# Moving the right-hand SBUF pools by 128 bytes and reordering the join between the two feed-forward products

## The chip, the cores and the metric

The kernel runs on one core of one Trainium2 chip. The metric is the device time of one execution, in microseconds. Three runs of the kernel before took 2131.59, 2133.08 and 2135.07 us; their median is 2133.08 us. The profiled execution was a run of its own: it took 2139.03 us, with a span of 2137.2 us from the first to the last instruction and a mean granted TensorE clock of 0.988.

## The reference

One layer of a decoder trunk over 512 positions and 2048 channels, all in float32: a conditioned RMSNorm, a mixer of three branches (causal pooling, forgetting attention with 8 heads, a gated linear recurrence), a residual; then a second conditioned RMSNorm, a gated feed-forward part with a causal convolution of width 3, a residual, and a last RMSNorm. Cut to what matters here:

```python
h = rmsnorm(x, g_ffn) * (1.0 + sc2) + sh2
g = causal_dwconv(h @ w_ffn_gate, ffn_conv_w, ffn_conv_b)   # 2048 -> 5632
a = silu(g) * (h @ w_ffn_up)                                # 2048 -> 5632
x = x + gt2 * (a @ w_ffn_down)                              # 5632 -> 2048
return rmsnorm(x, final_g)
```

## The kernel before

Channels lie on the 128 partitions, the 512 positions on the free axis. D is 16 tiles of 128 channels, the feed-forward width 44 tiles (NFF). Each float32 product is made of three matmuls of a rounded high part and a low part (mm3, lines 111 to 114): high weight by high data, high weight by low data, low weight by high data. So every weight tile that a DMA brings is split first: ScalarE (ACT) writes the high part, VectorE (DVE) the low one (split_w, lines 98 to 104).

**Stages.** (1) start(): the first norm while the conditioning weights stream in, and the first products, whose weight tiles raw_s hold several column groups side by side: columns from 0 for zs, the column group from SA = 416 (1664 bytes) for zb and zc, and for the later half of the channels a second part, split into a tile of its own, again for zc. (2) A list of slots run by drive() (line 247): each slot loads one weight tile two slots ahead, splits it one slot ahead and multiplies 16 channel tiles, 48 matmuls of 512 columns: queries and keys (z_q, z_k), values (zv, 256 columns), the output projection (z_o), and the first four gate and up tiles (z_b, z_g, z_u). (3) strassen(): feed-forward tiles 4 to 43, each as seven half-size products of 8 channel tiles with 256 columns (pair_steps, line 974), software-pipelined: the steps of tile p carry the end of tile o before it (results c21, c11, c12, then conv0, conv, silu, gated, store). Each gated tile is written to DRAM (a_d). (4) The second product down: four groups of 9, 13, 9 and 13 gated tiles (FFG), each group 16 slots. A slot multiplies its group's tiles (27 or 39 matmuls of 512 columns; in the last group twice 39 of 256) and adds the result to the residual x1 (down_done, line 1066). The gated tiles come back from DRAM (load_a into four ar buffers) and are split into the pool fa (split_a, line 1083). The first slot of the group has its weight split in one piece (FirstDown, tiles fd_raw, fd_h, fd_l).

**Memory.** Pools with side "right" are laid from the top of the partition downwards, the others from the bottom upwards. On the right lie, from the top: pad (32 bytes, which take 64), then in stages 1 and 2 xy and wp (raw weights and their halves wh, wl); in stage 3 in their place q, ring (the halves of the Strassen weights) and sm; in stage 4 fa (the halves of the gated tiles). On the left lie hp (the halves hh, hl of the normed data), the Strassen forms t3 and t42, mp (convolution results cv and gated tiles ac), and in stage 4 fd, wq (the weights of down and their halves), ar and xq (x1). By the addresses that the program gives them, all large left tiles start 64 bytes above a multiple of 256, all large right tiles 192 above one. A pool that takes the place of another is opened with reuse_waits="tile": a new tile waits for the last readers of the old tiles under it.

**What orders the work.** Each engine works through its own list in order. The lists come from a scheduler of the framework that simulates the program, so two instructions of one engine can change places against the text of the kernel where neither needs the other. All loads and stores are issued by one engine's queue (SyncE, SP), in order too: an issue that waits holds up those behind it.

**The join.** At the end of strassen() the chain of the last tile runs: c12 after the last product, conv0 (ACT), two conv steps (DVE), silu (ACT), gated (DVE), store (SP). Then the pools of stage 3 are closed, those of stage 4 opened, and the program reads:

```python
down[0].once("load")
raws = [load_a(i) for i in range(4)]
down[0].once("split0")
for i in range(FFG[0]):
    split_a(0, i, raws.pop(0))
    if i + 4 < FFG[0]:
        raws.append(load_a(i + 4))
for j in range(KC):
    x1[j] = xy.tile([P, S], F32, tag="xy", name=f"x1b_{j}")
    nc.sync.dma_start(x1[j], x1_d[j])
```

Of the kernel before, what the change touches and what calls it, by code (L numbers as in the profile page):

```python
# [10 lines left out]
F32 = mybir.dt.float32  # L11
# [5 lines left out]
P = 128  # L17
D = 2048
S = 512
KC = D // P  # L20
DFF = 5632
NFF = DFF // P
# [27 lines left out]
def trunk(ctx: ExitStack, tc: tile.TileContext, xT, c_d, pack_d, small_w, w_ada, w_s0, w_s1, w_b, w_z, w_v, w_o, w_gu, w_dn, out):  # L50
    nc = tc.nc
# [5 lines left out]
    def pool(stack, name, bufs, side="left"):  # L57
        return stack.enter_context(tc.tile_pool(name=name, bufs=bufs, side=side, reuse_waits="tile"))

    hp = pool(hps, "hp", 16)  # L60

    pool(ctx, "pad", 1, "right").tile([P, 8], F32, name="pad")
    xy = pool(rps, "xy", 16, "right")
    wp = pool(rps, "wp", 3, "right")
    dr = ctx.enter_context(tc.tile_pool(name="dr", bufs=1, space=bass.MemoryType.DRAM))
# [8 lines left out]
    def par(name, i=0, n=1):  # L74
        a = PACK[name][0] + i
        return pk[:, a:a + n]
# [12 lines left out]
    x1_d = [dr.tile([P, S], F32, name=f"x1_d{j}") for j in range(KC)]  # L89
# [81 lines left out]
    class Norm:  # L171
# [21 lines left out]
        def sum(self):  # L193
            nb = self.n // P
            s2 = bank(f"s2_{self.name}")

            for n, t in enumerate((self.acc, self.sq)):
                for b in range(nb):
                    T.matmul(s2[:, b:b + 1], t[:, b * P:(b + 1) * P], ones[:, 0:1], start=n + b == 0, stop=n == 1 and b == nb - 1)
            v, q, r = (self.tp.tile([P, 4], F32, tag=f"n{n}", name=f"{n}_{self.name}")[:, 0:nb] for n in "vqr")  # L200
            A.activation(q, s2[:, 0:nb], AF.Sqrt, bias=epsc, scale=1.0 / D)
            V.tensor_scalar(v, s2[:, 0:nb], 1.0 / D, EPS, op0=ALU.mult, op1=ALU.add)
            V.reciprocal(r, q)

            V.tensor_tensor(q, r, r, ALU.mult)
            V.tensor_tensor(q, q, v, ALU.mult)
            V.tensor_scalar(q, q, -0.5, 1.5, op0=ALU.mult, op1=ALU.add)
            V.tensor_tensor(r, r, q, ALU.mult)
            self.d = self.tp.tile([P, 4, P], F32, tag="d", name=f"d_{self.name}", bufs=1)[:, 0:nb]
            V.tensor_tensor(self.d, ident.unsqueeze(1).broadcast_to([P, nb, P]), r.unsqueeze(2).broadcast_to([P, nb, P]), ALU.mult)  # L210
# [36 lines left out]
    def drive(slots):  # L247
        def ahead(i, what):
            if i < len(slots):
                slots[i].once(what)  # L250

        ahead(0, "load")
        ahead(1, "load")
        ahead(0, "split0")
        ahead(0, "split1")
        yield
        for i, s in enumerate(slots):
            ahead(i + 2, "load")
            ahead(i + 1, "split0")
            if sum(x.n <= 1024 for x in slots[i:i + 3]) == 3:  # L260
                ahead(i + 3, "load")
                ahead(i + 2, "split0")
            for n in range(max(s.ada, 1)):
                if n < s.ada:
                    next(bg, None)
                ahead(i + 1, "split1")
            s.mm(s)
            for f in s.pe:
                f()
            for f in s.post:  # L270
                f()
# [382 lines left out]
    def later(f, *a):  # L654
        return lambda: f(*a)
# [60 lines left out]
    x1 = [None] * KC  # L716
    tm = Branches()
# [52 lines left out]
    def store_a(i, a):  # L770
        nc.sync.dma_start(a_d[i], a)
# [65 lines left out]
    def form1(c):  # L837

        v, h, l = x1[c][:, LO], g_h[c][:, HI], g_l[c][:, HI]
        A.copy(h, v)  # L840
        V.tensor_tensor(l, v, h.bitcast(F32), ALU.subtract)
# [11 lines left out]
    slots[-2].pe += [later(forms, c) for c in todo]  # L853


    sps = ExitStack()
    st = Branches()

    def strassen_start():

        rps.close()
        st.q = pool(sps, "q", 1, "right")
        st.r = pool(sps, "ring", 4, "right")
        st.m = pool(sps, "sm", 2, "right")
        f = st.first = Pair(PLAIN)
        f.load_a()
        f.load_b()
        f.sum1()
        f.high("a11")
        f.sum2()  # L870
        f.low("a11")
        f.high("s2")
        f.sum3()
        for c in range(HC):
            form1(c)

    class Pair:
# [10 lines left out]
        def load_a(self):  # L888
            self.load_part("a11", 0, 0, 1)
            self.load_part("a21", 1, 0, 2)  # L890
            self.load_part("a22", 1, 1, 2)
# [52 lines left out]


        def conv0(self):
            self.t = tm.m.tile([P, S], F32, tag="t", name=f"cv{self.i}")
            A.activation(self.t, self.g, AF.Identity, bias=par("fcb", self.i), scale=par("fcw", 3 * self.i + 2))

        def conv(self, s):  # L950
# [4 lines left out]
            A.activation(self.t, self.t, AF.Silu)  # L955

        def gated(self):
            self.a = tm.m.tile([P, S], F32, tag="a", name=f"ac{self.i}")
            V.tensor_tensor(self.a, self.u, self.t, ALU.mult)

    def b_of(j0, c):
# [12 lines left out]
    def pair_steps(p, q, o):  # L974

        A_, B_, C_, D_ = None, None, None, None
        q.load_a()
        A_ = p.half("A")
        p.product(A_, "a11", b11, True)
        p.high("s1")  # L980
        p.low("s2")
        o.c21()
        o.c11()

        o.last()
        m1 = p.kept("m1", A_)
        p.high("s3")
        p.low("s1")
        o.gated2()

        p.product(A_, "s2", T2, False)
        p.high("a12")
        o.c12()
        p.low("s3")
        o.conv0()
        o.conv(1)
        o.store2()

        C_ = p.half("C")
        p.product(C_, "s1", t1, True)  # L1000
        u2 = p.kept("u2", A_)
        p.high("a22")
        o.conv(2)
        o.silu()
        p.low("a12")
        p.sum4()

        p.product(A_, "s3", T3, False)
        q.load_b()
        q.high_a11()  # L1010
        p.low("a22")
        q.sum1()
        o.gated()

        B_ = p.half("B")
        p.product(B_, "a12", b21, True)
        u3 = p.kept("u3", A_)
        p.high("s4")
        q.sum2()
        q.low_a11()  # L1020
        o.store()

        D_ = p.half("D")
        p.product(D_, "a22", T4, True)
        q.high_s2()
        p.result("u", HI, u3, C_)
        p.low("s4")
        q.sum3()

        def last():  # L1030
            p.product(C_, "s4", b22, False)
        p.last = last
        p.c21 = lambda: p.result("u", LO, u3, D_)
        p.c11 = lambda: p.result("g", LO, m1, B_)
        p.c12 = lambda: p.result("g", HI, u2, C_)
        p.gated2 = p.store2 = lambda: None
        p.store = lambda: store_a(p.i, p.a)

    ABSENT = Absent()
# [2 lines left out]
    Pair.high_s2 = lambda self: self.high("s2")  # L1042

    def strassen():
        o, p = ABSENT, st.first
        for i in range(PLAIN, NFF):
            q = Pair(i + 1) if i + 1 < NFF else ABSENT
            pair_steps(p, q, o)
            o, p = p, q
        o.c21()  # L1050
        o.c11()
        o.last()
        o.c12()
        o.conv0()
        o.conv(1)
        o.conv(2)
        o.silu()
        o.gated()
        o.store()


    a_h, a_l = {}, {}
    down = []
# [19 lines left out]
    def split_a(g, i, a):  # L1083
        t = tm.fa.tile([P, 2, S], F32R, tag=f"a{g % 2}", name=f"a{i}", bufs=FFG[g])
        A.copy(t[:, 0], a)
        V.tensor_tensor(t[:, 1], a, t[:, 0].bitcast(F32), ALU.subtract)
        a_h[i], a_l[i] = t[:, 0], t[:, 1]
# [57 lines left out]
    for _ in stream:  # L1145
        pass
    strassen_start()
    strassen()

    sps.close()  # L1150
    fps.close()
    hps.close()
    ops = ExitStack()
    tm.fd = pool(ops, "fd", 1)
    wp = pool(ops, "wq", 3)
    tp = pool(ops, "tq", 2)
# [1 line left out]
    xy = pool(ops, "xq", 16)  # L1158
# [3 lines left out]
        norms[3, i] = Norm(tp, HALVES[i], f"n3{i}")  # L1162
    down_slots()
    stream = drive(down)
    down[0].once("load")
    raws = [load_a(i) for i in range(4)]
    down[0].once("split0")
    for i in range(FFG[0]):
        split_a(0, i, raws.pop(0))
        if i + 4 < FFG[0]:  # L1170
            raws.append(load_a(i + 4))
    for j in range(KC):
        x1[j] = xy.tile([P, S], F32, tag="xy", name=f"x1b_{j}")
        nc.sync.dma_start(x1[j], x1_d[j])
    for _ in stream:
        pass
    fas.close()
    n = norms[3, 1]
    n.sum()
    n.spread()  # L1180
    with tc.tile_pool(name="op", bufs=1, side="right", reuse_waits="tile") as op:
        o = op.tile([P, KC, S // 2], F32, name="o")
        for j in range(KC):
            V.scalar_tensor_tensor(o[:, j], x1[j][:, n.c], par("final_g", j), n.r, op0=ALU.mult, op1=ALU.mult)
            if j + 1 in OUT_CUTS:
                a = OUT_CUTS[OUT_CUTS.index(j + 1) - 1]
# [66 lines left out]
```

## Time and profile before

| | |
|---|---|
| median of three runs | 2133.08 us |
| profiled execution | 2139.03 us, span 2137.2 us |
| TensorE (PE) busy | 2064.7 us, 97% of the span |
| weight loads of PE (PEld) busy | 1858.5 us, 87% |
| VectorE (DVE) busy | 1503.1 us, 70% |
| ScalarE (ACT) busy | 862.3 us, 40% |
| DMA | 354.59 MB, mean 166 GB/s |
| Strassen stage | about 801 to 1604 us |
| second product | about 1614 to 2121 us |

Matmuls are pipelined, so the duration of one in the profile is longer than the distance from its start to the next one's start; the pace is the distance between starts. Times in the views are microseconds from the span's start. In a timeline the bracket behind an instruction tells how long its engine sat idle before it, and what released it.

### The profile page before, as it was taken

The page shows a single profiled execution, that of the slowest core. Times are in us where ns is not written, and L with a number is a line of the kernel's source. Part 1 is how long each engine was busy: PE and PEld are TensorE (multiplying, and loading weights), DVE is VectorE, ACT ScalarE, POOL GpSimd, SP SyncE. Part 2 cuts the span into 40 slices and gives each one's busy share as a digit, 9 for nine tenths or more (in the row PEclk, how much of TensorE's full clock was granted, in tenths as well). Part 3 has the DMA queues.
Part 4 walks back from the last instruction along what each step waited for, and adds up shares of the span by engine and source line. Part 5 has one row for each costly group of instructions (what it writes and reads, how often), then busy time and mean ns, then how long its engine had stood idle before and what let it go on. Part 6 is the DMA issues. An engine that isn't in the chain of part 4 may idle for free.

```text
span 2137.2 us, 31894 instructions
## 1 busy us (share of the span) xinstructions
PE 2064.7 (97%) x13172; PEld 1858.5 (87%) x13172; DVE 1503.1 (70%) x1901; ACT 862.3 (40%) x1196; POOL 29.5 (1%) x51
## 2 busy tenths in 40 slices
PE   5899999999999899999999999999997999999997
PEld 3678888988888689999999999999995888888997
DVE  7987876676677848888888888888865342343675
ACT  4247433235222634444444444444444231222442
POOL 0001100002000000000000000000000000000000
PEclk9999999999999899999999999999998999999998
DMA  9962465556888314443443443343328342333563
GB/s 360 363 232 90 177 225 210 217 217 220 287 308 304 107 55 143 124 126 108 124 130 106 121 133 107 120 131 109 123 65 293 103 157 89 94 123 109 189 210 129
DMA packets 86212, 354.59 MB, mean 166 GB/s; under 512 B 9393, under 2 KB 13617, under 8 KB 68529
## 3 DMA queue, kind: packets, MB, share of 16 engines
q1 hardware_dynamic: 86066, 352.55, 49.1%
q8 instruction: 103, 1.69, 0.3%
q14 instruction: 43, 0.35, 0.1%
HBM read 332.59 MB, written 19.92 MB: 165 GB/s over the span
## 4 chain that ended last, share of the span: by engine, by line
PE 86%; DVE 5%; DMA 5%; issue 2%; ACT 2%; SPq 0%; POOL 0%; DVEq 0%; ACTq 0%; POOLq 0%
PE z_d L112 8%; PE z_d L114 8%; PE z_d L113 8%; PE A L929 5%; PE A L928 5%; PE A L930 5%; PE C L928 4%; PE C L929 4%; PE C L930 4%; DMA raw_ada<-in_w_ada 3%; PE D L929 2%; PE B L929 2%; PE D L928 2%; PE B L928 2%; PE B L930 2%
## 5 line engine op out<-in xcount | busy, mean ns | idle before, releaser
L112 PE MATMUL z_d<-a,wh_d 128*128 128x512 f32 (+1 forms) x903 | 310.8, 344 | 4.1 <-ACT wh_d L102 4.1
L113 PE MATMUL z_d<-a,wh_d 128*128 128x512 f32 (+1 forms) x903 | 310.1, 343 | 0.0
L114 PE MATMUL z_d<-a,wl_d 128*128 128x512 f32 (+1 forms) x903 | 310.1, 343 | 0.0
L103 DVE TENSOR_TENSOR wl_d<-raw_d,wh_d 128x896 fp32r<-128x896 f32 (+3 forms) x158 | 145.1, 919 | 159.5 <-ACT wh_d L102 158.9
L102 ACT CAST wh_d<-raw_d 128x896 fp32r<-128x896 f32 (+3 forms) x158 | 127.0, 804 | 319.5 <-PE z_d L113 312.9
L112 PEld LDWEIGHTS z_d<-a,wh_d 128*128 128x128 f32 x903 | 170.2, 189 | 26.9 <-ACT wh_d L102 4.6
L114 PEld LDWEIGHTS z_d<-a,wl_d 128*128 128x128 f32 x903 | 170.1, 188 | 22.7 <-DVE wl_d L103 0.4
L113 PEld LDWEIGHTS z_d<-a,wh_d 128*128 128x128 f32 x903 | 170.3, 189 | 22.3
L125 DVE SCALAR_TENSOR_TENSOR raw_ada<-raw_ada,crep 128x2048 f32<-128x2048 f32 x64 | 146.4, 2288 | 60.5 <-DMA raw_ada<-in_w_ada 60.3
L1066 DVE SCALAR_TENSOR_TENSOR x1b<-z_d,mod,x1b 128x512 f32<-128x512 f32 (+1 forms) x80 | 51.5, 644 | 96.0 <-PE z_d L114 95.9
L928 PE MATMUL C<-hh_b,s1h 128*128 128x256 f32 x320 | 90.2, 282 | 2.9 <-ACT s1h L914 2.9
L930 PE MATMUL A<-hh_b,a11l 128*128 128x256 f32 x320 | 90.2, 282 | 1.7 <-DVE a11l L919 1.7
L928 PE MATMUL A<-t42h,s2h 128*128 128x256 f32 x320 | 90.1, 282 | 0.0
L929 PE MATMUL A<-t42l,s2h 128*128 128x256 f32 x320 | 90.1, 281 | 0.0
L928 PE MATMUL C<-hh_b,s4h 128*128 128x256 f32 x320 | 90.1, 281 | 0.0
L930 PE MATMUL C<-hh_b,s1l 128*128 128x256 f32 x320 | 90.0, 281 | 0.0
L928 PE MATMUL A<-t3h,s3h 128*128 128x256 f32 x320 | 90.0, 281 | 0.0
L929 PE MATMUL A<-t3l,s3h 128*128 128x256 f32 x320 | 90.0, 281 | 0.0
L930 PE MATMUL A<-t3h,s3l 128*128 128x256 f32 x320 | 90.0, 281 | 0.0
L928 PE MATMUL B<-hh_b,a12h 128*128 128x256 f32 x320 | 90.0, 281 | 0.0
L929 PE MATMUL B<-hl_b,a12h 128*128 128x256 f32 x320 | 90.0, 281 | 0.0
L930 PE MATMUL B<-hh_b,a12l 128*128 128x256 f32 x320 | 90.0, 281 | 0.0
(637 smaller groups left out, 6172.5 us busy)
## 6 DMA issues: line engine op xcount, KB each, us to landing
a<-in_w_gu SPq DMA_DIRECT2D x160, 512.0 KB, 3.9
raw_ada<-in_w_ada SPq DMA_DIRECT2D x64, 1024.0 KB, 5.2
raw_d<-in_w_dn SPq DMA_DIRECT2D x48, 832.0 KB, 4.4
ada<-in_w_ada SPq DMA_DIRECT2D x32, 1024.0 KB, 7.2
raw_d<-in_w_dn SPq DMA_DIRECT2D x31, 576.0 KB, 3.8
raw_o<-in_w_o SPq DMA_DIRECT2D x16, 1024.0 KB, 5.0
a_d<-ac SPq DMA_DIRECT2D x44, 256.0 KB, 3.8
ar<-a_d SPq DMA_DIRECT2D x44, 256.0 KB, 3.9
```

The lines of the kernel that those rows point to most:

```text
L102: A.copy(h, raw[:, a:b])
L103: V.tensor_tensor(l, raw[:, a:b], h.bitcast(F32), ALU.subtract)
L112: T.matmul(acc, wh, xh, start=start, stop=False)
L113: T.matmul(acc, wh, xl, start=False, stop=False)
L114: T.matmul(acc, wl, xh, start=False, stop=stop)
L125: V.scalar_tensor_tensor(raw, raw, 1.0, crep, op0=ALU.mult, op1=ALU.mult, accum_out=modr[:, n:n + 1])
L928: T.matmul(o, wh[:, w], xh, start=first, stop=False, skip_group_check=True)
L929: T.matmul(o, wh[:, w], xl, start=False, stop=False, skip_group_check=True)
L930: T.matmul(o, wl[:, w], xh, start=False, stop=last, skip_group_check=True)
L1066: V.scalar_tensor_tensor(x1[j][:, c], acc[:, c], mod[:, 80 + j:81 + j], x1[j][:, c], op0=ALU.mult, op1=ALU.add)
```

## The change

The padding tile at the top of the right side grows from 32 to 160 bytes (64 to 192 as laid out), which puts xy, wp and fa 128 bytes lower against a multiple of 256. A pool end (three tiles of 2048 bytes: g, u and t of the last feed-forward tile) is opened on the right ahead of the Strassen pools and stays open to the end of stage 4, and a second pad of 128 bytes lies below it during stage 3, so that q, ring and sm are 6400 bytes lower than before, 25 times 256. The last tile's gated result is written over its convolution tile t. strassen() ends with the last product and its results; the rest of the last chain (conv0 to store) is called after the loads and splits of the second product's first slots. The second slot's load and splits, and the third slot's load, are called among the splits of the first nine gated tiles. Four of the 16 residual tiles are loaded ahead of the last chain, and each of the other twelve at the end of a slot, three slots ahead of its use.

```diff
-    pool(ctx, "pad", 1, "right").tile([P, 8], F32, name="pad")
+    pool(ctx, "pad", 1, "right").tile([P, 40], F32, name="pad")
...
-    sps = ExitStack()
+    sps, ops = ExitStack(), ExitStack()
...
         rps.close()
+        st.end = pool(ops, "end", 1, "right")
+
+        pool(sps, "pad2", 1, "right").tile([P, 32], F32, name="pad2")
         st.q = pool(sps, "q", 1, "right")
...
         def conv0(self):
-            self.t = tm.m.tile([P, S], F32, tag="t", name=f"cv{self.i}")
+            if not hasattr(self, "t"):
+                self.t = tm.m.tile([P, S], F32, tag="t", name=f"cv{self.i}")
...
         def gated(self):
-            self.a = tm.m.tile([P, S], F32, tag="a", name=f"ac{self.i}")
+            self.a = tm.m.tile([P, S], F32, tag="a", name=f"ac{self.i}") if self.i + 1 < NFF else self.t
...
             q = Pair(i + 1) if i + 1 < NFF else ABSENT
+            if q is ABSENT:
+                for n in "gut":
+                    setattr(p, n, st.end.tile([P, S], F32, name=f"last_{n}"))
             pair_steps(p, q, o)
             o, p = p, q
+        o.last()
+        o.c11()
         o.c21()
-        o.c11()
-        o.last()
         o.c12()
-        o.conv0()
-        o.conv(1)
-        o.conv(2)
-        o.silu()
-        o.gated()
-        o.store()
+        return o
...
+    def load_x1(j):
+        x1[j] = xy.tile([P, S], F32, tag="xy", name=f"x1b_{j}")
+        nc.sync.dma_start(x1[j], x1_d[j])
+
     down[0].once("load")
     raws = [load_a(i) for i in range(4)]
     down[0].once("split0")
+    down[1].once("load")
     for i in range(FFG[0]):
         split_a(0, i, raws.pop(0))
         if i + 4 < FFG[0]:
             raws.append(load_a(i + 4))
-    for j in range(KC):
-        x1[j] = xy.tile([P, S], F32, tag="xy", name=f"x1b_{j}")
-        nc.sync.dma_start(x1[j], x1_d[j])
+        if i == 2:
+            down[2].once("load")
+        if i == 4:
+            down[1].once("split0")
+            down[1].once("split1")
+    for j in range(4):
+        load_x1(j)
+    for f in (last_pair.conv0, later(last_pair.conv, 1), later(last_pair.conv, 2), last_pair.silu, last_pair.gated, last_pair.store):
+        f()
+    for j in range(4, KC):
+        down[j - 3].post.append(later(load_x1, j))
```

## Rows read from the trace of the kernel before

**Rows 1.** Head of the profile page.
```profile
span 2137.2 us, 31894 instructions
```
**Rows 2.** Stretches: length; busy PE, PEld, DVE, ACT, POOL; clock; DMA share; GB/s.
```profile
1610.00:1620.00 10.00, 5.74 (x14) 4.25 (x15) 5.24 (x7) 3.66 (x8) 0.00 (x0) 0.52 0.88 300
```
**Rows 3.** PE timeline at the join: start, duration, engine, line, operation.
```profile
1603.56 0.28 PE L930 MATMUL C<-hh_b,s4l 128*128 128x256 f32 x1
...
1614.26 0.80 PE L112 MATMUL z_d<-a,fd_h 128*128 128x512 f32 x1 [10.42 <-ACT a L1085]
...
1615.58 0.63 PE L114 MATMUL z_d<-a,fd_l 128*128 128x512 f32 x1
...
1619.42 0.46 PE L114 MATMUL z_d<-a,fd_l 128*128 128x512 f32 x1
...
1628.74 0.80 PE L112 MATMUL z_d<-a,wh_d 128*128 128x512 f32 x1 [4.14 <-ACT wh_d L102]
...
1637.15 0.40 PE L112 MATMUL z_d<-a,wh_d 128*128 128x512 f32 x1
```
**Rows 4.** Timeline of ACT, then of DVE, at the join.
```profile
1608.95 1.15 ACT L1096 CAST fd_h<-fd_raw 128x1152 fp32r<-128x1152 f32 x1 [0.23 <-DMA fd_raw<-in_w_dn]
1613.59 0.62 ACT L1085 CAST a<-ar 128x512 fp32r<-128x512 f32 x1 [3.48 <-DMA x1b<-x_d]
...
1603.88 0.42 DVE L943 TENSOR_TENSOR g<-u,C 128x256 f32<-128x256 f32 x1 [2.43 <-PE C L930]
...
1610.14 1.36 DVE L1097 TENSOR_TENSOR fd_l<-fd_raw,fd_h 128x1152 fp32r<-128x1152 f32 x1 [0.69 <-ACT fd_h L1096]
1614.24 2.50 DVE L1086 TENSOR_TENSOR a<-ar,a 128x512 fp32r<-128x512 f32 x4 [2.75 <-ACT a L1085]
...
1623.13 0.69 DVE L1086 TENSOR_TENSOR a<-ar,a 128x512 fp32r<-128x512 f32 x1 [0.65 <-ACT a L1085]
```
**Rows 5.** Timeline of SP's issues at the join.
```profile
1595.33 6.97 SPq L1080 DMA_DIRECT2D ar<-a_d  x4
1603.87 0.33 SPq L1092 DMA_DIRECT2D fd_raw<-in_w_dn  x1
...
1609.47 0.32 SPq L771 DMA_DIRECT2D a_d<-ac  x1
...
1621.68 1.61 SPq L108 DMA_DIRECT2D raw_d<-in_w_dn  x3
```
**Rows 6.** PE timeline: matmuls 1, 7, 13 of zc, then zs.
```profile
101.83 0.39 PE L112 MATMUL zc<-hh_a,wh_s 128*128 128x512 f32 x1
...
103.22 0.39 PE L112 MATMUL zc<-hh_a,wh_s 128*128 128x512 f32 x1
...
104.58 0.40 PE L112 MATMUL zc<-hh_a,wh_s 128*128 128x512 f32 x1
...
107.37 0.39 PE L112 MATMUL zs<-hh_a,wh_s 128*128 128x512 f32 x1
```
**Rows 7.** DVE timeline: end of a slot of down, and four slots later.
```profile
1656.26 0.75 DVE L1066 SCALAR_TENSOR_TENSOR x1b<-z_d,mod,x1b 128x512 f32<-128x512 f32 x1 [1.69 <-PE z_d L114]
...
1681.46 0.75 DVE L1066 SCALAR_TENSOR_TENSOR x1b<-z_d,mod,x1b 128x512 f32<-128x512 f32 x1 [1.69 <-PE z_d L114]
```
**Rows 8.** Stretches as in rows 2: output projection; middle of Strassen.
```profile
525.00:700.00 175.00, 173.51 (x751) 140.52 (x749) 122.14 (x124) 45.53 (x55) 0.00 (x0) 1.00 0.84 294
...
900.00:1000.00 100.00, 100.00 (x845) 100.00 (x844) 82.40 (x91) 47.59 (x61) 0.00 (x0) 1.00 0.39 120
```
**Rows 9.** PE timeline: first of six 256-column matmuls; the next other one.
```profile
276.79 0.28 PE L112 MATMUL o<-pth,vh 128*128 128x256 f32 x1
...
277.49 0.28 PE L112 MATMUL sc<-k1h,qh 128*128 128x256 f32 x1
```
**Rows 10.** PE and SP timeline ahead of the Strassen stage.
```profile
789.99 0.39 PE L112 MATMUL z_u<-hh_b,wh_u 128*128 128x512 f32 x1
...
795.27 2.68 SPq L885 DMA_DIRECT2D a<-in_w_gu  x4
```

More of the change, by code (lines that the diff above doesn't have):

```diff
@@ L1147, in trunk @@
     strassen_start()
-    strassen()
+    last_pair = strassen()
     sps.close()
@@ L1152, in trunk @@
     hps.close()
-    ops = ExitStack()
     tm.fd = pool(ops, "fd", 1)
```

## The prediction, made before the change was run

> **What bounds the kernel now.** I read the page first, then stretches of the span with the granted clock, then PE's timeline wherever PE was not busy, and last the pace of its matmuls. The page has PE busy for 97% of a span of 2137.2 us [rows 1], so only two things can pay: the places where PE waits, and the pace at which its matmuls start. One long wait lies beside the change, the join of the Strassen stage and the second product: PE is busy for 5.74 of 10 us at a granted clock of 0.52 (the lower of its two levels, 1.2 GHz, nearly throughout) [rows 2]. The last Strassen matmul starts at 1603.56, the first of the second product at 1614.26 after 10.42 us of idling, its second slot at 1628.74 after another 4.14 us, and the third slot at 1637.15 [rows 3]. From there on PE doesn't wait: a slot of 27 matmuls ends every 6.3 us [rows 7]. The join thus takes 33.6 us for 54 matmuls; at the pace further on, (1681.46 - 1656.26) / 108 = 0.2333 us, these need 12.6. So 21.0 us are lost: 14.6 idle, and most of the rest to matmuls at 1.2 GHz, which start every (1619.42 - 1615.58) / 9 = 0.427 us [rows 3].
>
> Why PE waits: the first split of a gated tile starts only at 1613.59, though its load was issued from 1595.33 on [rows 4, 5]. The view names a residual load as releaser; that can't be the cause, since the split doesn't read it. By the layout the first fa tile lies over the last gated tile, which the store issued at 1609.47 is still reading [rows 5]: the split waits for c12, conv0, two conv steps, silu, gated, store and its landing, 4.1 us after the issue. The second idle time is the second slot's weights: the three slot loads are issued only at 1621.68, behind residual and gated-tile loads [rows 5].
>
> **The change part by part.**
>
> *The join.* The last tile's g, u and t move to a pool above fa, so no fa tile lies over them, and the chain conv0 to store leaves the path. What is late next is the first slot's own weight: fd_raw lies over normed data that the last product reads, is issued at 1603.87, right behind the last matmul, and its high half is ready at 1608.95 + 1.15 = 1610.1 [rows 3 to 5]. The first gated tile can be split earlier (its load is out, and the Strassen form that fa's first tile now overlaps is read last by the product before the last). So PE starts at 1610.1. Its clock has fallen by then, as before; it rose again 5.2 us after the restart (1614.26 to about 1619.5) [rows 3], so 12 matmuls go at 0.427. The third matmul waits some 0.55 us for fd_l (1.36 us after the high half, rows 4). The second slot's load now goes out behind fd_raw, so its 4.14 us and its own second spell at 1.2 GHz go. Slot 3 then starts at 1610.1 + 5.2 + 0.55 + 42 x 0.2333 = 1625.7 instead of 1637.15: **-11.5 us**. Best case, no slow spell and no wait: 1610.1 + 12.6 = 1622.7, -14.5. Worst: the gated tiles are split one by one as before, from 1614.24 to 1623.82, 9.6 us [rows 4], starting after fd_l's turn, so slot 1 ends near 1621.5; with a wait of 4.1 and a slow spell of 2.1 still ahead of slot 2, slot 3 starts at 1634: -3.
>
> The moved chain still has to run, some 5.2 us on ACT and DVE in turn (from 1604.30, the end of c12, to the store at 1609.47, rows 4 and 5), beside splits on two engines that are busy 3.66 and 5.24 of 10 us there [rows 2]; its tile is needed only in the last group. By the program's text it now stands behind twelve splits on ACT and DVE, and its store behind three slot loads, nine gated-tile loads and four residual loads on SP. If its store sits early in SP's list, the loads behind it wait for gated, as now. The DMAs of the join are three slot loads of 0.58 MB, five gated tiles and four residual tiles of 0.26 MB each, 4.1 MB in all: at the 300 GB/s of rows 2 14 us from 1604, to 1618, and the last of them is needed in slot 3 at 1625.7. Twelve residual loads behind slots instead of one burst: each has three slots (19 us) until its use, against the 5.1 us in which fd_raw's load came [rows 4, 5]. Nothing, for all of these.
>
> *128 bytes.* Is the pace of a matmul tied to where its operands lie? The trace holds the comparison. In the later half of the first stage zc runs 12 matmuls with weight columns from byte 1664 (13 x 128) of a right tile, then 12 with a tile from its own start: data from the same pool, whose tiles all lie alike, into the same banks, one after the other. By the layout the first 12 have weights and data at one remainder by 256, the others 128 apart. After six matmuls of settling (0.232 each), the first kind starts every (104.58 - 103.22) / 6 = 0.2267 us, the second every (107.37 - 104.58) / 12 = 0.2325 [rows 6]; the eight such rounds agree. The second product, with weights left and data right, goes at 0.2333 [rows 7]: so neither the weights' place nor the data's alone does it. The change puts wp (weights) on the left side's remainder in stage 2, and fa (data) in stage 4.
>
> The Trainium skill has a rule against this: "SBUF — State Buffer", section "Who interferes with whom", gives PE two independent read ports, one for the moving operand and one for the weights, and says PE never waits on anyone. By it the move is worth nothing and the sum is the join alone. Rows 6 contradict it here.
>
> Stage 2 has 2064 matmuls of 512 columns in its slots. 1296 outside the output projection x 0.0058 = 7.5 us, less a tenth for settling after scores and transposes: 6.8. In the output projection (768; 4.5 us) PE is busy for 173.5 of 175 us, but DMA moves 294 GB/s at a share of 0.84 [rows 8], so I count half: 2.2. Together **-9.0**. Second product: 31 x 3 x 16 = 1488, less the 54 of the join, x 0.0066: **-9.5**.
>
> The 2016 matmuls with 256 columns that change too (768 of zv, 1248 of the last group) have no clean row. Strassen, 128 apart, runs 845 in 100 us, 0.1183 [rows 8]; the six of attention, mostly at one remainder, take 0.70 / 6 = 0.117 [rows 9]. Between nothing and the same share as at 512 (2.5%, 5.9 us) I take half of that small difference: **-1.3**.
>
> ACT and DVE read the moved tiles too; I count nothing, since PE waits for them for only 1.5 us in the 175 of rows 8. Strassen's own pools move by 25 x 256, so its pace stays. But its first load now lies over weights that z_u reads for half of its slot, 789.99 + 24 x 0.2325 = 795.6, against the issue at 795.27 [rows 10]: **+0.3**.
>
> Sum: -11.5 - 9.0 - 9.5 - 1.3 + 0.3 = -31.0 us. The profiled execution took 2139.03, so 2108.0; the median of the runs lies 5.95 lower, so **2102 us**.
>
> **The rivals.**
>
> *The pads do nothing, 2122 us.* The fast dozen of rows 6 could have a period of 512 bytes instead of 256: there the weights lie 128 higher, while the change moves a side 128 lower. That is the same remainder by 256 but 256 apart by 512, a distance that no matmul of the trace has (chance 0.2). Or the place doesn't matter, and another trait of zc's first dozen makes its pace (0.08). For both: only one distance was ever seen fast. Against: between the dozens only the weights' tile changes, and which tile of one pool the data come from. Then -11.5 + 0.3 is left: 2121.9. This is also the outcome by the Trainium skill's rule of independent ports; rows 6 are why its chance is small.
>
> *The join keeps its splits one by one, 2111 us.* The scheduler may put the splits behind fd's on ACT, and SP's issues behind a waiting store. For it: that is how the loads run now, one ar buffer freed per split [rows 4, 5]. Then -3 instead of -11.5, with the pads: 2110.6.
>
> *Slower: the new distance is the bad one, 2144 us.* If operands 256 apart by 512 collide, all 3552 matmuls of 512 columns lose. It decides against the join's 11.2 us from 11.2 / 3552 = 0.0032 us each, that is a mean pace above 0.236. If the bad distance costs as much as the good one gains, 2064 x 0.0058 + 1488 x 0.0066 = 21.8 us, so 2122 + 22 = 2144. Against: no stretch of the trace holds a pace above 0.2333 at the full clock.
>
> **How the numbers follow.** Forecast (join and pads) 0.54, with a range of its own of 2095 to 2109; pads nothing 0.28; join little, pads right 0.08; slower rival 0.05; both little, near 2130, 0.05. A measurement of this kernel tells about 0.2% (4.3 us) from no change. The range takes in the forecast with the best join and gains at 256 columns below, and the pads' failure with a somewhat worse join above: 2094 to 2126. Faster by over 0.2% 0.90, within 0.2% 0.05, slower 0.05.
>
> **What would show it.** Join: the first z_d matmul about 6.3 us after the last Strassen one, released by fd_h, one spell at 1.2 GHz instead of two, no idle time ahead of slot 2, and slot 3 about 22 us after the last Strassen matmul (33.6 now). Pads: four slots of the second product take 108 x 0.2267 = 24.5 us instead of 25.2; z_q and z_k slots 10.9 instead of 11.2; zc's two dozens swap their paces. Strassen's pace unchanged. I am wrong if four slots keep 25.2 us, or if PE idles 10 us at the join again.

## The result, and the profile after

The changed kernel takes 2111.8 us (median of four runs, 2110.6 to 2116.6) against 2133.2 (2131.6 to 2135.1): a ratio of 0.9894, 95% interval 0.9874 to 0.9913. The forecast was 2102. Its profiled execution took 2111.69 us, that of before 2139.03. So the two profiled executions differ by 27.3 us (their spans by 27.7), where the prediction's sum had 31.0; the medians differ by 21.4.

Head of the page, then the stretch of the join as in [rows 2]:

```profile
span 2109.6 us, 31898 instructions
```
```profile
1600.00:1610.00 10.00, 6.31 (x20) 4.70 (x21) 7.99 (x12) 7.87 (x13) 0.00 (x0) 0.66 0.93 340
```

PE, ACT, DVE and SP at the join, as in [rows 3 to 5]:

```profile
1597.57 0.28 PE L933 MATMUL C<-hh_b,s4l 128*128 128x256 f32 x1
1603.69 0.80 PE L112 MATMUL z_d<-a,fd_h 128*128 128x512 f32 x1 [5.84 <-ACT fd_h L1099]
...
1604.81 0.79 PE L112 MATMUL z_d<-a,wh_d 128*128 128x512 f32 x1
...
1607.39 0.39 PE L112 MATMUL z_d<-a,fd_h 128*128 128x512 f32 x1
...
1617.92 0.39 PE L112 MATMUL z_d<-a,wh_d 128*128 128x512 f32 x1
```
```profile
1594.93 0.62 ACT L1088 CAST a<-ar 128x512 fp32r<-128x512 f32 x1 [3.69 <-PE D L932]
...
1602.49 1.15 ACT L1099 CAST fd_h<-fd_raw 128x1152 fp32r<-128x1152 f32 x1 [1.71 <-DMA fd_raw<-in_w_dn]
...
1598.23 2.56 DVE L1089 TENSOR_TENSOR a<-ar,a 128x512 fp32r<-128x512 f32 x4
```
```profile
1597.88 0.33 SPq L1095 DMA_DIRECT2D fd_raw<-in_w_dn  x1
1598.26 0.43 SPq L108 DMA_DIRECT2D raw_d<-in_w_dn  x1
...
1609.01 0.32 SPq L771 DMA_DIRECT2D a_d<-last_t  x1
```

The first split of a gated tile now runs ahead of the last Strassen matmul (1594.93; it was 10 us behind it), the first matmul of the second product starts 6.12 us after that matmul (10.70 before) and is released by fd_h, the store of the last gated tile goes out when nobody waits for it, and the third slot starts 20.35 us after the last Strassen matmul instead of 33.59. PE runs at 1.2 GHz once here (matmuls 0.43 apart until 1607.1) and has no second wait.

The pace, by how many matmuls lie in a stretch. In order: the second product before and after (512 columns), its last group before and after (256 columns, equally long stretches), the middle of the Strassen stage after. The columns are those of [rows 2]; a count takes in the one or two matmuls that only reach into the stretch, so the paces in the text are taken from the starts:

```profile
1660.00:1900.00 240.00, 240.00 (x1030) 193.06 (x1029) 90.77 (x115) 61.36 (x85) 0.00 (x0) 1.00 0.36 114
...
2000.00:2020.00 20.00, 20.00 (x171) 20.00 (x170) 12.55 (x18) 9.29 (x14) 0.00 (x0) 1.00 0.58 181
```
```profile
1660.00:1900.00 240.00, 240.00 (x1061) 198.72 (x1060) 93.12 (x118) 63.07 (x86) 0.00 (x0) 1.00 0.37 117
...
1960.00:1980.00 20.00, 20.00 (x169) 20.00 (x168) 12.25 (x17) 8.86 (x13) 0.00 (x0) 1.00 0.56 181
...
900.00:1000.00 100.00, 100.00 (x845) 100.00 (x845) 82.62 (x91) 47.86 (x61) 0.00 (x0) 1.00 0.39 119
```

At 512 columns a matmul starts every 226.67 ns instead of 233.33 (means of the start times in the trace), at 256 columns of the last group every 120.00 instead of 118.67: one became faster, the other slower. The Strassen stage keeps 845 per 100 us, as in [rows 8]. zc's dozens swapped their paces: between the starts that [rows 6] takes, 232.8 in the first and 227.0 in the second (seven of the eight rounds), where the trace of before has 227.6 and 232.6.

The stages, from starts of matmuls in the two traces (us; the Strassen stage ends with the start of its last matmul, the join with that of the third slot's first):

| stage | before | after | difference |
|---|---|---|---|
| start to first Strassen matmul | 801.14 | 790.32 | -10.83 |
| Strassen stage | 802.42 | 807.26 | +4.84 |
| join, to the third slot | 33.59 | 20.35 | -13.25 |
| second product, 512 columns | 334.60 | 325.04 | -9.56 |
| last group, 256 columns | 149.30 | 150.94 | +1.64 |
| tail | 16.20 | 15.69 | -0.51 |

The one stage that lost much is Strassen's, and it lost at its start. SP, then DVE and PE, after:

```profile
785.07 0.33 SPq L888 DMA_DIRECT2D a<-in_w_gu  x1
791.24 0.32 SPq L771 DMA_DIRECT2D a_d<-ac  x1
791.65 13.01 SPq L888 DMA_DIRECT2D a<-in_w_gu  x7
```
```profile
797.22 1.22 DVE L901 TENSOR_TENSOR s<-a,a 128x1024 f32<-128x1024 f32 x1 [4.88 <-DMA a<-in_w_gu]
...
800.83 0.58 PE L931 MATMUL A<-t42h,s2h 128*128 128x256 f32 x1 [5.56 <-ACT s2h L917]
```

In [rows 10] the first pair's four loads were issued together at 795.27, ahead of the fourth gated tile's store. Now only one stands ahead of it; the store waits until 791.24 for DVE's product, and the other three go out behind it. DVE waits 4.88 us for one of them, PE 5.56 us for what is made of it, and its next matmuls last 0.58 us, at 1.2 GHz. Before, the longest wait at this place was this one:

```profile
808.95 0.39 PE L928 MATMUL C<-hh_b,s1h 128*128 128x256 f32 x1 [2.85 <-ACT s1h L914]
```

Of the 4.84 us, 2.7 are the longer idle time and about 2 the 14 matmuls that ran at 1.2 GHz.

### The profile page after: what moved, and what is told of

It reads as the page before. It is cut to its first block, busy times and chain, and to the rows that moved or that the text cites. A ratio compares the mean times of both kernels' runs of the same rounds, so it can differ in the third digit from the quotient of the medians.

```text
span 2109.6 us, 31898 instructions
## 1 busy us (share of the span) xinstructions
PE 2044.0 (97%) x13172; PEld 1859.6 (88%) x13172; DVE 1502.4 (71%) x1901; ACT 862.8 (41%) x1196; POOL 30.0 (1%) x51
## 4 chain that ended last, share of the span: by engine, by line
PE 73%; DMA 1%; DVE 1%; ACT 0%; issue 0%; SPq 0%; DVEq 0%; ACTq 0%
PE z_d L112 8%; PE z_d L113 8%; PE z_d L114 8%; PE A L933 5%; PE A L932 5%; PE A L931 5%; PE C L931 4%; PE C L932 4%; PE C L933 4%; PE z_o L113 2%; PE z_o L112 2%; PE z_o L114 2%; PE B L931 2%; PE D L932 2%; PE D L931 2%; PE B L932 2%
## 5 line engine op out<-in xcount | busy, mean ns | idle before, releaser
L933 PE MATMUL A<-t42h,s2l 128*128 128x256 f32 x320 | 90.7, 283 | 0.0
L932 PE MATMUL C<-hl_b,s1h 128*128 128x256 f32 x320 | 90.2, 282 | 0.0
L931 PE MATMUL A<-hh_b,a11h 128*128 128x256 f32 x320 | 90.1, 281 | 0.0
L932 PE MATMUL C<-hl_b,s4h 128*128 128x256 f32 x320 | 90.1, 281 | 0.0
L932 PE MATMUL A<-hl_b,a11h 128*128 128x256 f32 x320 | 90.0, 281 | 0.0
```

Source lines behind the costliest of these rows:

```text
L931: T.matmul(o, wh[:, w], xh, start=first, stop=False, skip_group_check=True)
L932: T.matmul(o, wh[:, w], xl, start=False, stop=False, skip_group_check=True)
L933: T.matmul(o, wl[:, w], xh, start=False, stop=last, skip_group_check=True)
```

## The experiments

Each ratio is to runs of the kernel before that were timed beside the run in question; their medians lay between 2134.7 and 2138.0 us. Versions of different sets are therefore better compared by ratio, or by the stages of their traces, than by their medians.

### Before, once more

No edit.

> The kernel before once more, for its profile: the execution profiled first took 2139.03 us, 6 above the median of the timed runs, and the difference of the two profiles is 27.7 us where that of the medians is 21.4. Theory: the 6 us are an accident of that one execution (a clock spell or a late transfer), so the second profile has a span near 2131 and one of its stages is some 6 us shorter than in the first. Rival: a profiled execution of this kernel is always that much longer, span 2137 again with the same stages.

It took 2149.31 us, neither expectation's number. Its join and its stages before Strassen are those of the first profile within 2 us, but the Strassen stage took 812.21 us instead of 802.42, and this is its pace:

```profile
900.00:1000.00 100.00, 100.00 (x835) 100.00 (x835) 81.51 (x91) 47.58 (x60) 0.00 (x0) 1.00 0.36 117
```

835 matmuls per 100 us, not 845 [rows 8], from the first pair to the last: 120.00 ns instead of 118.67, at the full clock, for the same program at the same addresses. 1.33 x 6720 = 8.9 us; most of the other 0.9 is lost at the stage's start, where this execution ran 3.4 us at 1.2 GHz. In the first profile the starts repeat as 117, 122, 120, 119, 115 and so on, in the second as 123, 117, 120. So the stage has two steady rhythms, and each of these executions kept the one it fell into. This adds to the scatter of before (2131.6 to 2149.3 over all its runs). Why the first profile, which had the faster rhythm, lay 6 us above its median, no trace shows; against the later sets' medians of before (2134.7 to 2138.0) it lies only 1 to 4 us high.

### The pads alone, the join alone, and the second pad left out

```
pads_alone (before, with)              join_alone (after, with)
-  "pad" [P, 8]                        -  "pad" [P, 40]
+  "pad" [P, 40]                       +  "pad" [P, 8]
+  "pad2" [P, 32] ahead of q           -  "pad2"
no_pad2 (after, with)
-  "pad2"
```

> The two pads without the rest of the change. Theory: the 512-column matmuls run at 226.7 ns each as in the changed kernel; stages up to the Strassen products 10.8 us shorter than before, the first group of the second product 9.6 shorter, its last group (256 columns, now at equal remainder) 2.6 longer, and the Strassen start 4.8 longer, because the first gate loads again stand behind the store of the fourth gated tile on SyncE's queue (the shift by 256 bytes makes them wait for other tiles): together -12 to -14 us, 2119 to 2121. The join keeps its 33.6 us from the last Strassen matmul to the fourth slot and its two spells at 1.2 GHz. Rival: the stall at the Strassen start comes from the tile pool that the change puts at the end of the region and not from the pads: 2115 and an A stage as before.

Measured 2128.5 (ratio 0.9961, 0.9939 to 0.9982), its profiled execution 2127.8. In its profile the stages up to Strassen are 8.8 us shorter, the 512 columns of the second product 9.6 (325.04, as after), the last group 1.6 longer, the join unchanged but for 0.9. And the Strassen stage is 6.5 longer, with PE's wait of 6.2 us for s2h: the stall needs no new pool, so the rival falls. The gain of 8 us was less than expected, the spans' 11.2 nearly the expectation.

> The change without its two pads. Theory: every pace as before (232.4 to 233.3 ns for 512 columns, 118.67 for 256), the join 13 us shorter (20 us from the last Strassen matmul to the fourth slot, one spell at 1.2 GHz), the Strassen start 4.8 longer: -8.4 us, 2125. Rival: the join is shorter only because matmuls of slot 1 run at the faster pace, join -10 and no stall at the start: 2123; or the pads do everything and the join gives 3 us back later: 2130.

Measured 2130.2 (0.9969, 0.9955 to 0.9983). Join 20.11 us, one spell at 1.2 GHz; PE waits 5.9 us for s2h and the Strassen stage is 5.3 longer; all paces as before (334.60 and 149.28 us in the second product, 118.67 in Strassen). Span -9.0 us: the theory's parts, one by one. So with either half alone three loads stand behind the store (it goes out at 793.27 with the pads, at 801.49 with the join, one load ahead of it). That the moved tiles are what changed this order is argued, not tested.

> The changed kernel without the second pad: the Strassen weights then stand at the remainder of their data too. Theory: at 256 columns the equal remainder costs 1.3 ns a matmul (119.97 against 118.67, as in the last group of the second product), so the 6720 Strassen matmuls take 8.7 us more: 2120.5, the Strassen stage 816 us instead of 807. Rival: the 1.3 ns belong to that last group (its weights are split beside it) and not to the remainder: pace 118.67 and 2111.8. Second rival: an equal remainder is faster as with 512 columns, 118.67 to about 116: 2094.

Measured 2125.1 (0.9944, 0.9924 to 0.9963); Strassen stage 817.10 us.

```profile
900.00:1000.00 100.00, 100.00 (x836) 100.00 (x835) 81.71 (x90) 47.03 (x59) 0.00 (x0) 1.00 0.37 118
```

The pace is 120.00 ns: at 256 columns the equal remainder is slower than the fast rhythm at 128 bytes, as the last group said. But 120.00 is also the slow rhythm at 128, so this profile alone could not tell the address from the rhythm; the next one does.

### Bare rows of matmuls

```
for r in range(3):
    for n in (512, 256):
        for d in (0, 32, 64, 96, 128, 160, 192, 224, 256, 384):
            32 times:  acc += wh[d] xh;  acc += wh[d] xl;  acc += wl[d] xh
            one column of acc, copied into xh     # the next row waits for it
```

> Not the model: 96 matmuls in a row (32 weight blocks of 128 columns, each high part against the high and the low part of its data, each low part against the high) for each of ten distances from weights to data (0 to 384 bytes), at 512 and at 256 columns, the whole three times, each row of 96 begun anew after a stop of about 1 us; the output is not the reference's. Theory: at 512 columns the pace depends on the distance modulo 256 bytes: 226.7 ns at 0 and 256, about 233.3 at 128 and 384, the others between or at one of the two. At 256 columns it is 119.9 to 120.0 at 0 and 256, and at 128 and 384 the Strassen matmuls' 118.67, or 120.00 if the start of a row decides which of two rhythms it falls into, as the two profiles of the kernel before differ (118.67 in one, 120.00 in the other, with the same program): then the three rows at 128 bytes need not agree. Rival 1: the period is 512 bytes, and 256 is another pace than 0. Rival 2: distance alone does nothing, all rows of one width agree within 0.5 ns, and the paces of the kernel belong to its transfers and its splits beside them.

Stretches inside rows of the second round: 512 columns at 0, 128 and 256 bytes, then 256 columns at 0, 64 and 128 (length, PE busy with its matmuls, clock, DMA):

```profile
369.00:387.00 18.00, 18.00 (x81) 1.00 0.00 1
461.00:479.00 18.00, 18.00 (x79) 1.00 0.00 1
553.00:571.00 18.00, 18.00 (x81) 1.00 0.00 1
598.00:607.00 9.00, 9.00 (x78) 1.00 0.00 0
622.50:631.50 9.00, 9.00 (x82) 1.00 0.01 2
646.50:655.50 9.00, 9.00 (x78) 1.00 0.00 0
```

With no transfer and no other engine beside it PE keeps the kernel's paces within 0.1 ns, with one exception: the second product of before, 128 bytes apart, went at 233.33 where the bare row (and stage 2 of before) has 232.4. No run says why. Mean distance of starts in the last two thirds of a row (ns; the three rounds agree within 0.1 where one number stands):

| bytes | 0 | 32 | 64 | 96 | 128 | 160 | 192 | 224 | 256 | 384 |
|---|---|---|---|---|---|---|---|---|---|---|
| 512 columns | 226.67 | 233.33 | 233.33 | 234.3 | 232.4 | 233.3 | 228.9 | 233.33 | 226.67 | 232.3 |
| 256 columns | 120.00 | 118.34 | **113.33** | 118.65 | 118.65 | 120.04 | 117.8 | 116.7, 117.8, 117.8 | 120.00 | 118.69 |

Rows 256 bytes apart agree (0 and 256, 128 and 384), and the weights' address alone, with nothing else changed, moves the pace: theory right, both rivals wrong. The rows at 224 show two rhythms at one distance without a kernel around them; those at 128 agreed in all three starts. Nobody had expected the entry at 64: 256 columns run 5.3 ns faster there than in the Strassen stage.

> Not the model; the same bare rows of 96 matmuls, now at finer distances, with the low weights or the low data at another distance than the high ones, and at 384 and 128 columns; the output is not the reference's. Theory: the pace is a function of the column count and of each matmul's own distance modulo 256 bytes. So at 512 columns nothing between 0 and 48 bytes is faster than the 226.7 ns at 0; at 256 columns 48 to 80 bytes lie near the 113.3 of 64 bytes and 16 and 240 near the 120 of 0; with only one of the two weight parts 64 bytes off, two thirds or one third of the matmuls have the other distance and the mean lies between (256 columns: 115.6 and 117.8). Rival: the matmul before counts as well (its data and this one's weights are read together), and the mixed rows are not means of the plain ones.

At 256 columns only 64 gives 113.3: 48 gives 117.8, 56 117.8, 72 118.3, 80 118.7, and next best are 208 with 116.7 and 240 with 117.3; the theory had 113.3 from 48 to 80, and 120 at 16 (118.3) and 240. At 512, 240 bytes equal 0 (226.67), but 248 and 16 do not (233.3). High weights at 64 and low ones at 0 give 117.77 where the mean of the two would be 115.6 (the other way round it is 117.77 too, there the expected mean); high and low data 64 apart give 119.3. So the means of the theory don't hold: a matmul's neighbours count, as the rival has it (which of their reads meet is not shown), and no mixture tried here reached the pace of one common distance. At 384 columns 0 and 192 bytes are best (173.33; 176.7 at 64). Most rows of 128 columns ran at 1.2 GHz and tell nothing.

### The store behind the loads

```
 up_done:         -  store_a(i, a)
                  +  if i < PLAIN - 1: store_a(i, a)   else: tm.late = later(store_a, i, a)
 strassen_start:     f.load_b()
                  +  tm.late()
```

> The changed kernel with one edit: the store of the fourth gated tile is written behind the first pair's four loads. Theory: the stall at the Strassen start (PE waits 5.4 to 6.2 us for s2h in every kernel whose loads stand behind that store, DVE 4.7 to 5.5 for the load) is due to that order alone: the loads issue some 6 us sooner, the wait for s2h goes, the Strassen stage takes 802 to 804 us instead of 807, and the time falls by 3 to 5 us to 2107 to 2109. Rival: the loads wait anyway for the tiles whose place they take (released by the last splits and gates of the stage before): the wait stays above 4 us, 2111 to 2112.

Measured 2106.8 us (0.9860, 0.9842 to 0.9877, where the change has 0.9894).

```profile
782.76 1.76 SPq L892 DMA_DIRECT2D a<-in_w_gu  x4
788.93 0.33 SPq L771 DMA_DIRECT2D a_d<-ac  x1
```

The four loads go out together, the wait for s2h is gone, and the Strassen stage takes 802.53 us, that of before. Putting the order on one queue right gave back the whole 4.8 us, though not the same start: PE idles 1.3 and 1.8 us here instead of 1.7 and 2.9, and then runs 3.4 us at 1.2 GHz.

### Strassen weights 64 bytes above their data

```
-  pool(sps, "pad2", 1, "right").tile([P, 32], F32, name="pad2")
+  pool(sps, "pad2", 1, "right").tile([P, 48], F32, name="pad2")
```

> The changed kernel with one number changed: the second pad is 192 bytes instead of 128, so the Strassen weights stand 64 bytes (modulo 256) above their data instead of 128. Theory: the 6720 matmuls of 256 columns run at the 113.33 ns of the bare row instead of 118.67, 5.3 x 6720 = 35.9 us less: Strassen stage 771 us, 2076 in all. Rival 1: with three engines and transfers at work beside it the pace stays where it is, 118.67 or 120.00: 2112 to 2121. Rival 2: at that pace the splits on ScalarE and VectorE or the loads become the bound of a pair, and part of the gain goes: 2085 to 2100.

Measured 2080.5 us (four runs, 2078.2 to 2081.5; 0.9732, 0.9712 to 0.9753): 31 us off the changed kernel's median (35 by the two ratios) for 64 bytes of pad.

```profile
900.00:1000.00 100.00, 100.00 (x885) 100.00 (x884) 86.90 (x97) 50.39 (x64) 0.00 (x0) 1.00 0.38 124
```

That is 113.33 ns from start to start, the stage 771.21 us instead of 807.26 (36.0; 35.9 expected). DVE is busy for 87% of the stretch, and PE still does not wait for it.

### All of it, and the two groups of runs

```
 best:   store_late, with pad2 [P, 48]
 split_w: +  off: tiles of b - a + 64 columns, used from column off
 last group of down:  +  s.off = 16   # 64 bytes
 slots of v:          +  s.off = 48   # there the split weights are the data
 best_again: the same program       best_early: without store_late's edit
```

> The store behind the loads, the Strassen weights 64 bytes above their data, and the two other stages of 256 columns likewise: the split weights of the last group of the second product start 64 bytes into their tiles, and the split weights of the v slots (there they are the data) 192 bytes into theirs; slots grow by 256 bytes, so everything else keeps its remainder. Theory: from store_late's 2106.8, 35.9 less in the Strassen stage, 1248 x 6.6 ns = 8.2 in the last group, 768 x 6.5 = 5.0 in the v slots: 2058, between 2055 and 2064. Rival: the v slots and the last group are held by their splits or loads, not by the pace, and only the Strassen part comes: 2071.

Measured 2067.5, 2103.3, 2065.1, 2069.3, 2096.2 and 2093.4 us: median 2081.3 (ratio 0.970, 0.9656 to 0.9743, without the two longest), but in two groups some 30 us apart, at the same granted clock (0.99 in all six). The profiled one is of the lower: Strassen 767.16 us, last group 145.80 instead of 150.94, not the 8.2 us expected, since its first half runs at 117.78 ns and only the rest at 113.33:

```profile
1940.00:1960.00 20.00, 20.00 (x173) 20.00 (x172) 12.38 (x18) 9.32 (x14) 0.00 (x0) 1.00 0.55 175
2030.00:2050.00 20.00, 20.00 (x180) 20.00 (x178) 10.70 (x17) 7.54 (x11) 0.00 (x0) 1.00 0.20 70
```

The step lies at the one-column matmuls of a norm's sum that stand in PE's order there (eight in the trace). The v slots took both paces in turn, 115.9 ns on average instead of 119.9. The 3 us that this makes over 768 matmuls do not show: the first Strassen matmul starts at 791.8 us on average in the four profiles with this edit and at 791.7 in the five with the pads and without it. But there the data moved and the weights kept their place, so 113.3 goes with the distance and not with the weights' own address.

> The kernel 'best' once more, for its profile: its runs lie in two groups, 2065 to 2069 and 2093 to 2103 us, and the one profiled was of the first. Theory: at one distance the 256-column matmuls have more than one steady rhythm, and which one an execution falls into is settled where the stream restarts (after a stop, or where the clock returns to 2.4 GHz). If this execution is of the upper group, its Strassen matmuls run at 117.8 ns (4.4 x 6720 = 30 us more) or 118.7 (36 us) from the first pair to the last, with no other stage changed; if it is of the lower, at 113.33 as before. Rival: the 28 to 36 us are waits or a longer time at 1.2 GHz, and the pace is 113.33 either way.

2069.47 us, of the lower group, with the same paces at the same places: it could not show the upper one.

> As 'best', with the store ahead of the loads as in the changed kernel, so that the Strassen products begin with the stop of 5.6 us and the longer spell at 1.2 GHz after it. Theory 1: that start decides the rhythm (strassen64, with this start, had four of four runs within 2078 to 2081): all runs at 113.33, 2066 to 2074, above the fast runs of 'best' by the 4 us of the stall. Theory 2: the rhythm is a matter of chance at either start: some of the runs lie 28 to 36 us higher, near 2098 to 2106.

Measured 2074.9, 2072.1, 2100.7, 2071.6, 2070.6 and 2102.9: median 2073.5 (ratio 0.9727, 0.9679 to 0.9774, without the longest). Theory 2 is borne out: the stop at the start doesn't settle the rhythm.

```
 best_reset: best, with, after the second product of pairs 0 to 2 and the last group's first slot,
+  two one-column matmuls whose result nobody reads (in the trace four)
```

> As 'best', with two matmuls of one column (a norm's sum in kind, their result read by nobody) put in after the second product of each of the first three Strassen pairs, and once after the first slot of the second product's last group. In three profiles the last group began at 117.78 ns and went over to 113.33 right behind the eight such matmuls of the norm's sum, at the same place of the program. Theory: such a break settles the rhythm at 64 bytes to 113.33, so no run lies 28 to 36 us above the fastest (5 of 17 runs did with these weights at 64 bytes), the last group takes 143 us instead of 145.8, and the four breaks cost some 0.5 us each: 2064 to 2069 for all runs. Rival: a break throws the rhythm anew by chance, or only some breaks do: slow runs as often as in 'best' (2092 to 2104), and the last group still at 117.78 behind its break.

Measured 2095.3 to 2100.3 in all five runs (median 2097.1; 0.983, 0.9816 to 0.9843): the theory fell, and a profile now shows what a run of this length looks like. Around the first break the pace goes from 113.3 (the seven matmuls ahead of it) to 117.78 and stays there through the second and third break to the end of the stage, 798.32 us, 31.2 more than in best's profile:

```profile
800.99 0.28 PE L937 MATMUL A<-t42h,s2l 128*128 128x256 f32 x1
801.10 0.50 PE L986 MATMUL re<-ones,m 128*128 128x1 f32 x4
801.46 0.36 PE L935 MATMUL C<-hh_b,s1h 128*128 128x256 f32 x1
```
```profile
900.00:1000.00 100.00, 100.00 (x852) 100.00 (x851) 83.34 (x92) 47.98 (x61) 0.00 (x0) 1.00 0.40 122
...
1940.00:1960.00 20.00, 20.00 (x179) 20.00 (x178) 12.30 (x19) 9.21 (x13) 0.00 (x0) 1.00 0.61 202
2030.00:2050.00 20.00, 20.00 (x173) 20.00 (x172) 15.94 (x27) 8.79 (x14) 0.00 (x0) 1.00 0.89 273
```

In the last group the added break did bring 113.33 at once (179 in 20 us), and then the norm's sum, which had switched 'best' to the fast rhythm, switched this one to the slow. So a break can change the rhythm either way, or leave it as the second and third did; what decides is not shown. That the long runs of best and best_early come from the slow rhythm fits their size (4.45 x 6720 = 29.9 us) and is not shown, since none of them was profiled. Which event decides in an execution, and how to hold the fast rhythm, stays open.

Every run of every version with the Strassen weights at 64 bytes (2065.1 to 2103.3) beats every run of both kernels (2110.6 at best). strassen64 had no long run among four; best_early has the lowest median of the versions timed more than once (2073.5) and best the lowest run (2065.1), these two with 5 of 12 runs some 30 us up.

## Why the prediction was right, and by how much it missed

The mechanism was right: join and pads both pay, and they add once the stall that either of them brings to the Strassen start is counted once (spans -11.2 and -9.0, with 6.5 and 5.3 of stall in them; together -27.7, with 4.8). The time alone could not have told this: 2111.8 lies 9.7 us above the forecast, 10 below "pads nothing" and beside the 2111 of "splits one by one", and the range held all three. The stages and paces decide. By the prediction's steps, against the differences between the two profiles:

- **Join, -11.5: measured -13.25** (-13.5 alone). PE restarts 6.12 us after the last Strassen matmul, released by fd_h (the prediction says 6.3 among its signs, but its sum restarts at 1610.1, which is 6.54); one spell at 1.2 GHz, no idle time ahead of slot 2. The 1.75 us more: PE restarts 0.4 us sooner than in the sum; the first 12 matmuls take 4.6 us instead of 5.75, with 8 of them at the low clock instead of 12 and no wait for fd_l, since matmuls of the next slot are issued in between; and the other 42 take 0.2 less. The fear that the splits would stand behind a waiting store on SP was unfounded here; it came true at the other end of the Strassen stage.
- **512 columns, stage 2, -9.0: measured -10.8**, and -9.5 as the mean over all profiles with the pads against all without (first Strassen matmul at 788.3 to 795.3 in nine, 800.6 to 802.1 in three). The output projection gave 4.2 of its 4.5 us (180.36 to 176.13 from its first matmul to its last), where I had counted half; the -10.8 holds the v slots' loss, below.
- **512 columns, second product, -9.5: measured -9.56.** Period 256 bytes, the chance of 0.2 for 512 gone. The independent ports of the Trainium skill ("SBUF — State Buffer", "Who interferes with whom") would have the pads give nothing. The bare rows, where only the weights' address differs, contradict that: 226.67 ns at 0 bytes against 232.4 at 128.
- **256 columns, -1.3: wrong in sign.** Measured 118.67 to 120.00 in the last group (+1.64) and 118.6 to 119.9 in zv (+1.0). I had bounded it from nothing to a gain and left out a loss, though of the two rows I had, 0.1183 at 128 bytes is a count that takes in matmuls at the edges (the starts give 118.67) and 0.117, mostly at equal remainder, is a mean of six.
- **Strassen start, +0.3: measured +4.84.** Of the terms from the trace this is the one furthest off. I priced the first load's own delay and not the order on SP: a store that waits for DVE came ahead of three loads. The prediction had named just this danger, but for the join.
- **From the profile to the median, -5.95: not right.** The profiled execution after lies on its median, so the excess of the profile before doesn't carry over. The two profiled times differ by 27.3 us against the sum's 31.0, so of the miss of 9.7 us the terms make 3.7 and this transfer 6.0. That the terms miss by so little is in part luck: join and stage 2 came out 3.6 us better, the 256 columns of the last group and the Strassen start 7.5 worse. Two executions of one program can differ by 9 us in the Strassen pace alone, so a single profile's excess over a median is an accident to be left out, or kept as a bound.

The rivals: "pads nothing" and "slower" fall by the pace; "splits one by one" falls by the rows of the join.

## What to carry to other kernels

Before anything else is moved, read the pace of each kind of matmul from the trace, by column count, and compare it with a bare row over the distance of weights and data: here 64 bytes of pad were worth 36 us of the Strassen stage, more than the whole change. A pad or a new pool also moves everything below it, so look at what each queue's order becomes where the moved tiles are first filled. And where a steady pace can be one of two, one profile is one draw; count matmuls per stretch in a second one before explaining a difference.

## What the runs showed of the chip

- A matmul's pace depended on the distance of weights and data, the same at 0 and 256 and at 128 and 384 bytes, and the best distance tried on the columns: 0 or 240 for 512 (226.67 against 232.4 at 128), 0 or 192 for 384 (173.33 against 176.7 at 64), 64 for 256 (113.33 against 118.65 at 128 and 120.00 at 0). It is narrow: 8 bytes beside 64 lose most of it (117.8, 118.3).
- At one distance there can be two rhythms that hold for hundreds of microseconds: 118.67 and 120.00 at 128 bytes (the two profiles of before), 113.33 and 117.78 at 64. In best_reset a break of 0.36 us switched from one to the other, in the Strassen stage to the slower and in the last group to the faster; two more left it. At 0 bytes only one was seen (120.00 and 226.67).
- At the Strassen start idle times of 1.7 and 5.6 us were followed by 6.8 us at 1.2 GHz (after); 1.3 and 1.8 us by 3.4 us of it (store_late); 1.7 and 2.3 us by 3.4 in one profile of before, and 1.7 and 2.9 by none in the other.
